# Softmax row sums in an attention sweep: the third pair of probability tiles added on VectorE, and the products with ones run over one tile per batch

## The chip, the cores and the metric

The kernel runs on one core of a Trainium2 chip. The core has five engines with a queue each: TensorE (PE; its weight loads are shown apart as PEld), VectorE (DVE), ScalarE (ACT), GpSimd (POOL) and SyncE (SP), which issues transfers. Each queue works in order, and engines wait for one another through semaphores. The metric is device time in microseconds (us): the median over runs of the whole kernel, which is one launch.

## The reference

One layer of a hybrid backbone: a latent stream of 2048 tokens and a context of 256 tokens, width 1024, in float32. Attention has 8 query heads and 2 key/value heads of size 64; a gated linear recurrence has 4 heads; an output projection and a feed-forward block follow. The change touches the softmax of the latent attention alone:

```python
def latent_attention(qx, kx, vx, kc, vc):
    ...
    keys = jnp.concatenate([kc, kx], axis=1)
    vals = jnp.concatenate([vc, vx], axis=1)
    ...
    def block(q):
        s = jnp.einsum('bqkgd,bnkd->bkgqn', q, keys).astype(jnp.float32) * scale
        p = jax.nn.softmax(s, axis=-1)
        return jnp.einsum('bkgqn,bnkd->bqkgd', p.astype(vals.dtype), vals)
```

Each of 2048 x 8 query rows has 2304 keys. The kernel computes exponentials, multiplies them with the values, sums them per row, and divides at the end. The change is in how the row sums are made.

## The kernel before

The kernel runs in stages: modulation vectors, input projections, the attention sweep with the recurrence woven into it, the output projection, and the feed-forward block. The change lies in the sweep, which takes from about 734 to 1734 us of the profiled span.

**Items and slots.** An `Item` is 128 queries of one key/value group (4 heads, so 512 query columns); there are 32 items. The 2304 keys are 18 key tiles of 128 (`NKT` = 18). The loop at L1098 runs over slots `x`, one for each item and key tile: `n, k = divmod(x, 18)`. In a slot, `scores` computes the scores of one key tile (L1000 and L1001, 128 keys x 512 query columns, into one of three PSUM banks), and ScalarE takes their exponentials into one half of a pair tile `p` of 128x1024 (L1004), two key tiles to a pair. In the same slot `chunk` computes one piece of the score extremes that a later item needs (L969 or L975 on TensorE into one of two PSUM banks, then a minimum on VectorE at L971 or L977).

**Batches.** Six key tiles, which are three pairs, form a batch (`BATCH` = 6): 3 batches an item, 96 in all. In the fourth slot of a batch (`k % 6 == 3`) `add` has GpSimd add the first two pairs into the tile `ps` (L1011). The tile has one buffer. Eight slots after the batch's first one, `products` runs on TensorE: the products of the values with the six tiles (L1020, 12 products, two recorded passes each), accumulated in `av[:, :256]`; then the row sums (L1028), in which a 128x32 tile of ones, `one32`, is multiplied with four blocks of 128 columns for each half of a tile, accumulated in `av[:, 256:384]`. Four such products stand side by side on the array's columns, each on 32 of them. They run over two tiles per batch: the sum `ps`, and the third pair `p`. That is 16 products a batch, in the trace 32 passes. After an item's third batch, `drain` copies `av` out on ScalarE (L1034) and takes the reciprocal of the sums on VectorE (L1036), and `finish` scales the output and writes it to `s_att`.

**The recurrence.** `rec.step` and `rec.round` place the second half of the layer between the slots. A round has, for one or two lanes, small products on TensorE (L684, into `pa`), a masked copy on VectorE (L694), reductions on VectorE (L721), four products on GpSimd (L703, L706, L715, L717) and copies on ScalarE (L709, L710). The round's TensorE part goes ahead of a batch's `products` and its rest behind them (L1190 to L1199).

**The order of the work.** In the sweep the order on TensorE and VectorE is the order of the program text (`manual_schedule`, L1080 and L1159; SyncE too for the first item). The queues of ScalarE and GpSimd, and SyncE's from the second item on, are ordered by a planner that runs a time line of its own when the program is built. So an instruction on VectorE stands exactly where the loop places it, and whatever follows it there waits behind it, while ScalarE's and GpSimd's order may come out differently whenever the program changes.

Of the kernel before, what the change touches and what calls it, by code (L numbers as in the profile page):

```python
# [13 lines left out]
ALU = mybir.AluOpType  # L14
AX = mybir.AxisListType

P = 128
# [36 lines left out]
def rows_bcast(ap, n=P):  # L54

    return bass.AP(tensor=ap.tensor, offset=ap.offset, ap=[[0, n], [1, ap.size()]])
# [12 lines left out]
def block_kernel(ctx: ExitStack, tc: tile.TileContext, a: dict, out: bass.AP, dbg=None):  # L69
    nc = tc.nc  # L70
# [3 lines left out]
    def pool(stack, name, bufs=1, space=None, side=None):  # L74
        kw = dict(name=name, bufs=bufs, reuse_waits="tile", side=side)
        if space is not None:
            kw["space"] = space
        return stack.enter_context(tc.tile_pool(**kw))
# [70 lines left out]
    with ExitStack() as st:  # L149
# [11 lines left out]
        for j in range(8):  # L161
            wm = wmp.tile([P, KT, 256], F32, tag="wm", name=f"wm{j}")
            nc.sync.dma_start(wm, w_mod_r[:, :, j * 256:(j + 1) * 256])
            if j in DVE_MOD:
                for r in range(2):
# [5 lines left out]
                    for i in range(2):  # L171
                        nc.tensor.matmul(pcol[:, 2 * j + i, r:r + 1], acc[:, i * P:(i + 1) * P], ones,
                                         start=True, stop=True)
                continue
            pm = ps_m.tile([P, 512], F32, tag="mm", name=f"pm{j}", bufs=2)
            for k in range(KT):
                nc.tensor.matmul(pm[:2, :256], sc[:, k, :], wm[:, k, :],
                                 start=(k == 0), stop=(k == KT - 1))
# [7 lines left out]
        for r in range(2):  # L186
            for which in range(2):
                ks = slice(which * KT, (which + 1) * KT)
                nc.vector.tensor_tensor(modc[:, 2 * r + 1 - which, :], pcol[:, ks, r], bcol[:, ks],
                                        op=ALU.add)  # L190
# [21 lines left out]
    with ExitStack() as st:  # L212
# [40 lines left out]
        with ExitStack() as p1:  # L253
            ps_x = pool(p1, "ps_x", 4, PSUM)
            xh = pool(p1, "xh", 2)
            for gr in list(range(1, NTOK // 256)) + [0]:
# [6 lines left out]
                b = (gr + 1) // 2  # L263
                o = (gr - 1) % 2 * 256 if gr else 0
# [18 lines left out]
                for kk in range(KT // 2):  # L283
                    pt = ps_x.tile([P, 512], F32, tag="t", name=f"xT{gr}_{kk}")
                    for i in range(2):
                        for j, xt in enumerate(xs):
                            k = 2 * kk + i
# [3 lines left out]
                    for i in range(2):  # L291
                        k = 2 * kk + i
# [317 lines left out]
    with ExitStack() as st:  # L610
# [4 lines left out]
        op = pool(st, "op", 1, side="right")  # L615
# [322 lines left out]
        NKT = NTOK // P  # L938
        BATCH = 6
        LAGT = 3  # L940

        class Item:
# [65 lines left out]
            def add(self, p):  # L1008

                t = self.sums[p // 3] = op.tile([P, 1024], F32, tag="ps", name=f"ps{self.nm}_{p}")  # L1010
                nc.gpsimd.tensor_tensor(t, self.pairs[p - 1], self.pairs[p], op=ALU.add)  # L1011

            def products(self, k0):

                if k0 == 0:
                    self.av = ps_av.tile([P, 512], F32, tag="av", name=f"av{self.nm}")
                for k in range(k0, k0 + BATCH):
                    for i in range(2):
                        o = k % 2 * 512 + i * 256
                        nc.tensor.matmul(self.av[i * 64:(i + 1) * 64, :256],  # L1020
                                         VS[:, k, self.g * 64:(self.g + 1) * 64],
                                         self.pairs[k // 2][:, o:o + 256],
                                         start=(k == 0), stop=(k == NKT - 1), skip_group_check=True)
                b = k0 // BATCH
                for n, t in enumerate((self.sums.pop(b), self.pairs[3 * b + 2])):
                    for o in range(0, 1024, 512):
                        for i in range(4):
                            nc.tensor.matmul(self.av[i * 32:(i + 1) * 32, 256:384], one32,  # L1028
                                             t[:, o + i * P:o + (i + 1) * P], start=False,
                                             stop=(b == 2 and n == 1 and o > 0), skip_group_check=True)  # L1030

            def drain(self):
                self.ot = op.tile([P, 256], F32, tag="ot", name=f"ot{self.nm}")
# [18 lines left out]
        one32 = kvp.tile([P, 32], F32, name="one32")  # L1052
# [9 lines left out]
        def load_kb(g, r):  # L1062
            n = NTOK // 3
            nc.sync.dma_start(f32v(KB[r][:64, :]), s_k[g][:64, r * n:(r + 1) * n])
# [4 lines left out]
        items = [Item(g * NCH + qt, qt, g) for g in range(2) for qt in range(NCH)]  # L1069
# [28 lines left out]
        for x in range(NKT * NIT + 1):  # L1098
            n, k = divmod(x, NKT)
            item = items[n] if n < NIT else None  # L1100
            if item is None:
                rec.begin(2 * NIT)
                assert not chunks and not rec.lanes and not rec.plan and rec.late is None
                items[-1].products(NKT - BATCH)
                items[-1].drain()
                items[-1].finish(ps_st, "s")
                border.close()
                hst.close()
                p5 = ctx.enter_context(ExitStack())
                ep = pool(p5, "ep", 3)  # L1110
                wop = pool(p5, "wop")
                wo = [[wop.tile([P, D], F32R, name=f"wo{w}{k}") for w in "hl"] for k in range(KT)]
                gate1 = wop.tile([P, D], F32, name="gate1")
                mp = pool(p5, "mp", 2)
                wsp = pool(p5, "wsp", 3)
                ps_y = pool(p5, "ps_y", 2, PSUM)
                ps_mt = pool(p5, "ps_mt", 2, PSUM)
                for k in range(KT):
                    ws = wsp.tile([P, D], F32, tag="ws", name=f"wos{k}")
                    nc.sync.dma_start(ws, a["w_out"][0, k * P:(k + 1) * P, :])  # L1120
                    nc.scalar.activation(wo[k][0], ws, AF.Copy)
                    (nc.vector if k in WOV else nc.gpsimd).tensor_tensor(
                        wo[k][1], ws, f32v(wo[k][0]), op=ALU.subtract)
                nc.sync.dma_start(gate1, rows_bcast(modrow[0, 2 * D:3 * D]))

                mixed = {}

                def mix_token(t):

                    rw = slice(t * P, (t + 1) * P)  # L1130
                    mx = mp.tile([P, D], F32, tag="mix", name=f"mix{t}")
                    for g in range(2):
                        nc.sync.dma_start(mx[:, g * 256:(g + 1) * 256].rearrange("p (c t) -> p c t", t=P),
                                          s_att[g][:, rw].rearrange("(c p) t -> p c t", p=P))
                    for h in range(NH):
                        nc.sync.dma_start(mx[:, 512 + h * P:512 + (h + 1) * P], s_hg[h][rw, :])
                    mh = mp.tile([P, KT, P], F32R, tag="mh", name=f"mh{t}")
                    ml = mp.tile([P, KT, P], F32R, tag="ml", name=f"ml{t}")
                    pt = ps_mt.tile([P, 512], F32, tag="t", name=f"mt{t}")
                    for i in range(4):  # L1140
                        nc.tensor.transpose(pt[:, i * P:(i + 1) * P], mx[:, 512 + i * P:512 + (i + 1) * P], ident)
                    for kk, (src, eng) in enumerate(((mx[:, :512], nc.gpsimd), (pt, nc.vector))):
                        pv = src.rearrange("p (k t) -> p k t", t=P)
                        nc.scalar.activation(mh[:, kk * 4:kk * 4 + 4, :], pv, AF.Copy)
                        eng.tensor_tensor(ml[:, kk * 4:kk * 4 + 4, :], pv,
                                          f32v(mh[:, kk * 4:kk * 4 + 4, :]), op=ALU.subtract)
                    mixed[t] = mh, ml

                mix_token(NCH // 2)
                break  # L1150
            if n == NCH - 1 and k in (8, 14):
                load_kb(1, k // BATCH - 1)
            if n == NCH and k == 0:
                load_kb(1, 2)
            if x == NKT:
                nc.sync.dma_start(f32v(KS[1]), s_k[1])
            if x == NKT:
                border.close()
                border.enter_context(tc.manual_schedule(engines={mybir.EngineType.PE, mybir.EngineType.DVE}))  # L1159
            if k == 6 and n + 2 < NIT:  # L1160
                items[n + 2].load()
            if k == 4 and n + 1 < NIT:
                items[n + 1].load_low()
            item.scores(k)
            if k == 3 and n:
                items[n - 1].drain()
            for m, c in chunks.pop(x, ()):
                items[m].chunk(c)
            if rec.late is not None:
                wait -= 1  # L1170
                if wait <= 0:
                    rec.flush()
            made = iter(())
            for hr, j in STEPS.get(k, ()):
                hr += 2 * n
                if j == 0 and hr:
                    rec.begin(hr)
                rec.step(hr, j)
                if (hr, j) in outputs:
                    wait = 3  # L1180
                if j != 5:
                    next(rec.beside, 0)
                else:
                    made = rec.round()
            if k == 13 and n + 1 < NIT:
                items[n + 1].maxima()
            if k == 5 and n:
                items[n - 1].finish(ps_h, "h")
            pending.append(made)
            if k % BATCH == LAGT - 1:  # L1190
                made = [m for m in pending]
                pending.clear()
                for m in made:
                    next(m, 0)
                y = x - LAGT + 1 - BATCH
                if y >= 0:
                    items[y // NKT].products(y % NKT)
                for m in made:
                    next(m, 0)  # L1199
# [593 lines left out]
```

## Time and profile before

| what | us |
|---|---|
| median of 3 runs | 3235.79 |
| lowest and highest of them | 3234.75, 3237.18 |
| profiled execution, its own time | 3230.49 |
| span of that execution | 3228.7 |
| mean granted TensorE clock in it | 0.993 |

The profiled execution is a run by itself, 5.3 us under the median; 1.8 us of its own time lie outside the span.

How to read the rows. A row of the busy times has for each engine the busy time, its share of the span and the number of instructions. A row of a stretch has its start and end, its length, and then for PE, PEld, DVE, ACT and POOL the busy time and the number of instructions; then the granted TensorE clock, the share of the DMA engines and GB/s. Where such a row is of one engine alone, it has that engine's busy time only. A row of a time line has the start, the time from its first start to its last end, the engine, the line, the operation, output and inputs with their shapes, and how many instructions are merged in it; in brackets stands idle time before it and what ended that. A row of waits names who waited for whom, the total, how often, and the longest. A row of one source line has the shortest, median and longest duration in ns. Names stand without buffer numbers: `ps` is the sum tile, `p` a pair, `mn` the minima, `mx` their scores, `pa` the recurrence's products, `one` the ones. TensorE's matmuls are pipelined, so that neighbouring rows of it overlap.

### The profile page before, as it was taken

Reading aid. Unit: us, or ns where it says so; the run is one execution under the profiler, and the core shown is the slowest. Engines: PE = TensorE matmul, PEld = TensorE weight load, DVE = VectorE, ACT = ScalarE, POOL = GpSimd, SP = SyncE. Lnnn points to the kernel's source line nnn. Section 1 sums busy time; section 2 is a strip of 40 time slices with the busy share of each in tenths; the row PEclk is TensorE's granted clock in tenths of the full one; section 3 lists DMA queues with packets and bytes.
Section 4 is the critical chain, followed back from the end, with each engine's and each line's share of the span. In section 5 each row is a group of like instructions: output and inputs, shape, how many; then the busy total and the mean of one; then the engine's idle time right before and its main releaser. Section 6 shows DMA issues by size and latency. Waiting matters only on the chain. (4 is left out here: it accounts for less than half of the span.)

```text
span 3228.7 us, 55815 instructions
## 1 busy us (share of the span) xinstructions
PE 3145.3 (97%) x21212; PEld 2559.5 (79%) x21212; DVE 1755.1 (54%) x3070; ACT 1326.6 (41%) x2563; POOL 1575.1 (49%) x1403
## 2 busy tenths in 40 slices
PE   8999999999999999999999999999999999999998
PEld 5998987896777777777777887888877778888886
DVE  6344555416666665665653656445458753333566
ACT  4422222215554555554543225333335443333344
POOL 4322222206767767776634226777600168776222
PEclk9999999999999999999999999999999999999999
DMA  7243544324111211211006435555575533332665
GB/s 246 92 137 125 153 145 146 119 93 121 31 36 46 67 34 49 59 37 48 28 21 201 134 115 183 196 179 189 173 291 195 193 111 115 108 104 98 243 195 185
DMA packets 368999, 406.86 MB, mean 126 GB/s; under 512 B 31285, under 2 KB 260889, under 8 KB 368346
## 3 DMA queue, kind: packets, MB, share of 16 engines
q1 hardware_dynamic: 368730, 403.30, 38.9%
q8 instruction: 166, 2.72, 0.4%
q14 instruction: 103, 0.84, 0.1%
HBM read 273.34 MB, written 129.78 MB: 125 GB/s over the span
## 5 line engine op out<-in xcount | busy, mean ns | idle before, releaser
L971 DVE TENSOR_REDUCE mn<-mx 128x1 f32<-128x512 f32 x496 | 333.9, 685 | 209.7 <-PE mx L969 204.6
L1004 ACT ACTIVATE p<-s 128x512 f32<-128x512 f32 x576 | 338.5, 598 | 167.3 <-PE s L1001 147.5
L1011 POOL TENSOR_TENSOR ps<-p,p 128x1024 f32<-128x1024 f32 x96 | 229.9, 2395 | 162.3 <-ACT p L1004 162.3
L1020 PE MATMUL av<-p,VS 128*64 128x256 f32 x2304 | 268.7, 382 | 0.0
L1000 PE MATMUL s<-qa,K 128*128 128x512 f32 x576 | 253.4, 440 | 10.8 <-ACT p L1004 10.8
L1001 PE MATMUL s<-qb,KB 128*128 128x512 f32 x576 | 227.4, 395 | 0.0
L1020 PEld LDWEIGHTS av<-p,VS 128*64 128x64 f32 x2304 | 158.9, 138 | 82.5 <-issue 13.9
L969 PE MATMUL mx<-K,qa 128*128 128x512 f32 x496 | 200.9, 406 | 2.7 <-DVE mn L971 2.4
L1621 DVE TENSOR_TENSOR dl<-dl,x 128x512 fp32r<-128x512 f32 x154 | 113.7, 761 | 70.8 <-ACT x L1614 69.9
L1000 PEld LDWEIGHTS s<-qa,K 128*128 128x128 f32 x576 | 109.0, 189 | 47.9 <-issue 19.8
L1614 ACT ACTIVATE x<-dl 128x512 fp32r<-128x512 f32 x154 | 96.2, 631 | 106.1 <-DMA dl<-s_hid0A 41.1
L1614 ACT ACTIVATE dh<-dl 128x512 fp32r<-128x512 f32 x154 | 89.0, 623 | 93.7 <-PE pd1A L1682 48.3
L345 PE MATMUL f<-hTh,wh 128*128 128x512 f32 (+1 forms) x320 | 120.8, 377 | 6.9 <-ACT ft L374 6.9
L969 PEld LDWEIGHTS mx<-K,qa 128*128 128x128 f32 x496 | 93.4, 188 | 41.4 <-DVE mn L971 17.8
L1621 DVE TENSOR_TENSOR dl<-dl,dh 128x512 fp32r<-128x512 f32 x154 | 102.0, 688 | 43.1 <-ACT dh L1614 42.0
L122 POOL TENSOR_TENSOR rs_xf<-ms_xf,mhalf 128x1 f32<-128x1 f32 x16 | 12.7, 803 | 227.6 <-DVE ms_xf L120 227.6
L345 PE MATMUL f<-hTh,wl 128*128 128x512 f32 (+1 forms) x320 | 118.5, 370 | 0.0
L345 PE MATMUL f<-hTl,wh 128*128 128x512 f32 (+1 forms) x320 | 118.4, 370 | 0.0
L1001 PEld LDWEIGHTS s<-qb,KB 128*128 128x128 f32 x576 | 109.6, 190 | 10.9
L1445 PE MATMUL pA<-x,A22h 128*128 128x512 f32 x352 | 108.9, 391 | 4.5 <-DVE r L1518 4.5
L1445 PE MATMUL pA<-x,A11h 128*128 128x512 f32 x352 | 110.7, 395 | 2.4 <-ACT A11h L1414 2.4
L1445 PE MATMUL pC<-x,A12h 128*128 128x512 f32 x352 | 112.0, 391 | 0.0
(373 smaller groups left out, 9337.0 us busy)
## 6 DMA issues: line engine op xcount, KB each, us to landing
w<-in_w_gu_dram SPq DMA_DIRECT2D x88, 512.0 KB
wm<-in_w_mod_dram SPq DMA_DIRECT2D x24, 1024.0 KB
dl<-s_wT SPq DMA_DIRECT2D x88, 256.0 KB
dl<-s_wB SPq DMA_DIRECT2D x66, 256.0 KB
wq<-in_w_down_dram SPq DMA_DIRECT2D x44, 256.0 KB
s_wT<-wq SPq DMA_DIRECT2D x44, 256.0 KB
dl<-s_hid1S SPq DMA_DIRECT2D x44, 256.0 KB
dl<-s_hid0S SPq DMA_DIRECT2D x44, 256.0 KB
```

The lines of the kernel that those rows point to most:

```text
L122: nc.gpsimd.tensor_tensor(rs, ms, mhalf[:, :width], op=ALU.pow)
L345: nc.tensor.matmul(pm[:, :n], w[wi][:, k, c0:c0 + P], hT[b][hi][:, k, :], start=(k == 0 and i == 0), stop=(k == KT - 1 and i == 2))
L969: nc.tensor.matmul(s, self.qa[:, h * P:(h + 1) * P], K[:, k * 512:(k + 1) * 512], start=True, stop=True)
L971: nc.vector.tensor_reduce(self.mn[:, h, k:k + 1], s, axis=AX.X, op=ALU.min)
L1000: nc.tensor.matmul(s, KS[self.g][:, ks], self.qa, start=True, stop=False)
L1001: nc.tensor.matmul(s, KB[k // BATCH][:, k % BATCH * P:(k % BATCH + 1) * P], self.qb, start=False, stop=True)
L1004: nc.scalar.activation(self.pairs[p][:, o:o + 512], s, AF.Exp, scale=-1.0)
L1011: nc.gpsimd.tensor_tensor(t, self.pairs[p - 1], self.pairs[p], op=ALU.add)
L1020: nc.tensor.matmul(self.av[i * 64:(i + 1) * 64, :256], VS[:, k, self.g * 64:(self.g + 1) * 64], self.pairs[k // 2][:, o:o + 256], start=(k ...
L1445: nc.tensor.matmul(acc, w[wi][:, k, :], x[xi][k], start=(start and k == 0 and i == 0), stop=(stop and k == KH - 1 and i == 2), skip_group_ ...
L1614: nc.scalar.activation(hi, f32v(lo), AF.Copy)
L1621: nc.vector.tensor_tensor(lo, f32v(lo), f32v(hi), op=ALU.subtract)
```

## The change

A method `add_last` adds the third pair to the sum tile in place, on VectorE. `products` then runs the ones products over that one tile: 8 products a batch instead of 16. In the loop `add_last` is placed in slots with `k % 6 == 1`, behind the slot's `scores` and `chunk` and ahead of the recurrence's step; for a batch whose first slot is k0 that is slot k0 + 7, one slot ahead of its `products`. For the last item's last batch it stands directly ahead of `products` behind the loop. The tiles, their buffers and all other instructions stay.

```diff
+            def add_last(self, p):
+
+                t = self.sums[p // 3]
+                nc.vector.tensor_tensor(t, t, self.pairs[p], op=ALU.add)
+
             def products(self, k0):
...
                 b = k0 // BATCH
-                for n, t in enumerate((self.sums.pop(b), self.pairs[3 * b + 2])):
-                    for o in range(0, 1024, 512):
-                        for i in range(4):
-                            nc.tensor.matmul(self.av[i * 32:(i + 1) * 32, 256:384], one32,
-                                             t[:, o + i * P:o + (i + 1) * P], start=False,
-                                             stop=(b == 2 and n == 1 and o > 0), skip_group_check=True)
+                t = self.sums.pop(b)
+                for o in range(0, 1024, 512):
+                    for i in range(4):
+                        nc.tensor.matmul(self.av[i * 32:(i + 1) * 32, 256:384], one32,
+                                         t[:, o + i * P:o + (i + 1) * P], start=False,
+                                         stop=(b == 2 and o > 0), skip_group_check=True)
...
                 assert not chunks and not rec.lanes and not rec.plan and rec.late is None
+                items[-1].add_last(NKT // 2 - 1)
                 items[-1].products(NKT - BATCH)
...
             for m, c in chunks.pop(x, ()):
                 items[m].chunk(c)
+            if k % BATCH == 1 and x > BATCH:
+                items[(x - 2) // NKT].add_last((x - 2) % NKT // 2)
             if rec.late is not None:
```

## The prediction

> **What bounds the kernel now.** I read the page's busy times and its chain of waits first, then the table by stretches for the attention sweep, then its groups of instructions.
>
> ```profile
> PE 3145.3 (97%) x21212; PEld 2559.5 (79%) x21212; DVE 1755.1 (54%) x3070; ACT 1326.6 (41%) x2563; POOL 1575.1 (49%) x1403
> 734.00:1734.00 1000.00, 975.51 (x10051) 727.90 (x10051) 597.31 (x1067) 515.49 (x1042) 678.65 (x715) 0.99 0.18 53
> DVE mn L971 <- PE mx L969: 188.3, 106, 4.0
> POOL ps L1011 <- ACT p L1004: 162.3, 51, 8.6
> PEld s L1000 <- ACT p L1004: 16.4, 17, 2.8
> PE s L1000 <- ACT p L1004: 10.8, 8, 2.4
> PEld mx L969 <- DVE mn L971: 15.5, 38, 1.0
> ```
>
> The second row is the whole sweep, from 734 to 1734 us: TensorE is busy for 975.5 of 1000 us at a granted clock of 0.99, VectorE for 597, ScalarE for 515, GpSimd for 679. The last five rows are waits of that stretch (total, times, longest). VectorE and GpSimd mostly wait for work that TensorE leads; TensorE's own waits are small: 27 us for ScalarE's exponentials, 15.5 us for VectorE's minima. So TensorE's instruction stream sets the length of this stage, and time taken out of it counts, unless another engine then becomes late.
>
> **What is removed.** Per batch, eight products of `one32` with the third pair: 16 recorded passes.
>
> ```profile
> L1028 PE MATMUL av<-ps,one x1536: 272/273/298, 743.5 to 1733.6; 128*32 128x128 f32 x192
> L1028 PE MATMUL av<-p,one x1536: 272/273/273, 744.0 to 1734.0; 128*32 128x128 f32 x192
> 743.53 0.64 PE L1028 MATMUL av<-ps,one 128*32 128x128 f32 x16
> 744.00 0.62 PE L1028 MATMUL av<-p,one 128*32 128x128 f32 x16
> 744.54 0.50 PE L1000 MATMUL s<-qa,K 128*128 128x512 f32 x1
> ```
>
> 1536 / 16 = 96 batches. The passes overlap (273 ns each, but 16 of them in 0.62 us), so a group is priced from its start to the next group's start. The step from the group over the sum tile to the group over the third pair is 0.46 to 0.47 us here and in the rows below; the next step, 0.54 us, also holds the change back to the wide score product, which stays. I take 0.46: 96 x 0.46 = **44.2 us** off TensorE.
>
> **What is added.** 96 additions of 128x1024 on VectorE, both inputs in SBUF. Weight preparation after the sweep has the same shape:
>
> ```profile
> L1122 DVE TENSOR_TENSOR wol<-wos,woh x4: 1225/1226/2959, 1720.1 to 1737.6; 128x1024 fp32r<-128x1024 f32 x4
> 1720.12 2.96 DVE L1122 TENSOR_TENSOR wol<-wos,woh 128x1024 fp32r<-128x1024 f32 x1 [6.89 <-ACT woh L1121]
> 1719.62 5.71 POOL L1122 TENSOR_TENSOR wol<-wos,woh 128x1024 fp32r<-128x1024 f32 x2
> ```
>
> 1.23 us undisturbed, so 96 x 1.23 = 118 us of VectorE's 403 idle us. One of the four took 2.96 us: it began while GpSimd was in a subtraction over SBUF. So the price has two ends, 1.23 us alone and 2.96 us behind such an operation.
>
> [...]
>
> **Where the addition lies in a usual batch.** It stands on VectorE behind the minimum of slot k0 + 7 and ahead of that of slot k0 + 8 (k0 is the batch's first key tile). This is a whole batch on three engines:
>
> ```profile
> 1361.54 0.40 PE L969 MATMUL mx<-K,qa 128*128 128x512 f32 x1
> 1362.26 0.50 PE L969 MATMUL mx<-K,qa 128*128 128x512 f32 x1
> 1362.69 1.17 PE L684 MATMUL pa<-Q,M 128*64 128x64 f32 x32
> 1363.69 2.76 PE L1020 MATMUL av<-p,VS 128*64 128x256 f32 x24
> 1366.38 0.64 PE L1028 MATMUL av<-ps,one 128*32 128x128 f32 x16
> 1366.84 0.62 PE L1028 MATMUL av<-p,one 128*32 128x128 f32 x16
> 1367.96 0.39 PE L969 MATMUL mx<-K,qa 128*128 128x512 f32 x1
> ...
> 1361.52 1.97 DVE L971 TENSOR_REDUCE mn<-mx 128x1 f32<-128x512 f32 x3
> 1363.90 0.74 DVE L694 COPY_PREDICATED A<-mask,pa 128x512 f32<-128x512 int32 x1 [0.41 <-PE pa L684]
> 1365.30 0.67 DVE L721 TENSOR_REDUCE T<-T 128x256 f32<-128x512 f32 x1
> 1368.39 0.69 DVE L971 TENSOR_REDUCE mn<-mx 128x1 f32<-128x512 f32 x1 [2.42 <-PE mx L969]
> ...
> 1363.47 0.65 POOL L715 TENSOR_TENSOR Q<-Q,T 128x256 f32<-128x256 f32 x1 [2.93 <-PE pa L684]
> 1368.90 2.40 POOL L1011 TENSOR_TENSOR ps<-p,p 128x1024 f32<-128x1024 f32 x1
> 1363.47:1371.30 7.83, 7.83 (x9) 1.00 0.00 0
> ```
>
> Two of the three minima are done at 1361.52 + 2/3 x 1.97 = 1362.83. GpSimd is idle there, so the addition runs to 1364.06. The ones products want it at 1366.38: 2.3 us to spare, under the value products of L1020. Queued behind it are the third minimum (then done at 1364.75) and the recurrence's masked copies and reductions, 2.07 us from 1363.90 to 1365.97 before and so to 1366.8 after. The next minimum is ready for VectorE at 1368.39, or 1367.93 with TensorE 0.46 us earlier. So 1.1 us remain: the addition costs nothing here. The cover is VectorE's 2.42 us wait during the products; with no cover it costs 1.23 - 0.46 = 0.77 us net per batch.
>
> GpSimd's L715 is held from 1363.47 to 1364.06, 0.6 us, and by the last row (a stretch of 7.83 us, all of it busy, in nine operations) its queue runs without a pause to the end of the next `ps` sum, which so comes 0.6 us later. What GpSimd does late, ScalarE and the next addition receive late.
>
> **Where it doesn't fit.** The addition needs GpSimd's sum of the first two pairs. By the wait row above, 51 of the 96 sums waited for exponentials; the other 45 started behind GpSimd's own queue. Two of those:
>
> ```profile
> 787.01 2.38 POOL L1011 TENSOR_TENSOR ps<-p,p 128x1024 f32<-128x1024 f32 x1
> 786.40 1.38 DVE L971 TENSOR_REDUCE mn<-mx 128x1 f32<-128x512 f32 x2
> 789.73 0.64 PE L1028 MATMUL av<-ps,one 128*32 128x128 f32 x16
> ...
> 1088.55 2.38 POOL L1011 TENSOR_TENSOR ps<-p,p 128x1024 f32<-128x1024 f32 x1
> 1090.89 0.86 POOL L715 TENSOR_TENSOR Q<-Q,T 128x256 f32<-128x256 f32 x1
> 1089.38 1.28 DVE L971 TENSOR_REDUCE mn<-mx 128x1 f32<-128x512 f32 x2
> 1090.58 0.76 DVE L694 COPY_PREDICATED A<-mask,pa 128x512 f32<-128x512 int32 x1
> 1092.43 0.18 DVE L721 TENSOR_REDUCE T<-T 128x16 f32<-128x32 f32 x1
> 1093.05 0.64 PE L1028 MATMUL av<-ps,one 128*32 128x128 f32 x16
> 1095.06 4.15 DVE L971 TENSOR_REDUCE mn<-mx 128x1 f32<-128x512 f32 x6 [2.45 <-PE mx L969]
> ```
>
> First one: the sum is done at 789.39, VectorE stands from 787.09, the addition ends at 790.62, and the ones products, wanted at 789.73, are 0.89 us late.
>
> Second one: VectorE is free at 1090.07, the sum is done at 1090.93, but GpSimd is already in L715 until 1091.75. The addition then ends at 1092.98, just in time for 1093.05. Behind it, though, stand a minimum (0.69) and the recurrence's work, 2.03 us from 1090.58 to 1092.61: done at 1095.7, where the next minimum was due at 1095.06 - 0.46 = 1094.6. VectorE is 1.1 us behind, and its six minima in 4.15 us are 0.69 us each, the same as TensorE's slot (the products for the minima of 1361.54 and 1362.26 above are 0.72 us apart), so it does not catch up before the next products. With two banks for the minima some 0.3 us of that is forgiven (4.15 / 6 a slot, two slots, less matmul and reduction): 0.8 us on TensorE.
>
> So such a batch costs 0 (the one at 1368.90 is also of the 45 and has its products as far off as the first batch shown) to 0.85 us, the mean of 0.89 and 0.8. All 45 would make 38 us. I take a third, 13 us, because most recurrence rounds leave the 2.4 us wait. The waits for exponentials (25 in all, 27 us) could each grow by GpSimd's 0.6 us: 0 to 15 us; I take 2, near the lower end, because GpSimd has its own pauses (162 us ahead of `ps`) in which such a delay ends. The first item has no output to drain and the last no minima; both go at the same price. At the end of the sweep the last addition may be held by L1122 on GpSimd (2.96 - 1.23 = 1.7 us, once); output projections fill TensorE there, so nothing. Transfers don't move.
>
> **Sum.** -44.2 + 13 + 2 = -29 us: the profiled span 3228.7 becomes 3200, its own time 3230.5 becomes 3201.5, and the median of the runs shown, 3235.8, becomes **3207 us**. With the bounds of the unknown terms, 0 to 53, the time lies between 3192 and 3245.
>
> **Rivals.** (1) Nothing is lost: 3235.8 - 44.2 = 3192. For it: 2.3 us to spare in the usual batch. Against: the 45 late sums.
>
> (2) A new wait takes the place of the products: all 45 late batches cost 0.85 us and the exponentials 2: -44.2 + 40 = -4, 3232, which can't be told from no change (0.2%, 6.5 us, is about what a measurement here can tell). For it: 0.89 us worked out at 789. Against: VectorE idles 40% of the stage.
>
> [...]
>
> **Chances.** Forecast 0.52 (its own range 3196 to 3226), rival 1 0.20, rival 2 0.11, rival 3 0.17. Rival 2 I count as 0.03 faster, 0.07 same, 0.01 slower; of the forecast's 0.52, a tail of 0.02 lies within 0.2%. Faster: 0.50 + 0.20 + 0.03 = 0.73; same 0.09; slower 0.18. The range runs from 3188, a little under rival 1, to 3244, the end of the bounds; most of rival 3 is left out.
>
> **What would show it.** [...] A TensorE wait for `ps` on VectorE of some 0.9 us in many batches would be rival 2. If the sweep shrinks by 44 us with the same waits, rival 1 holds. The forecast is wrong if the sweep's 1000 us shrink by less than 15.

## The result, and the profile after

The changed kernel takes 3237.89 us in the median of 12 runs (3229.09 to 3246.02), the kernel before 3235.28 in 12 runs beside it (3230.74 to 3241.61). The ratio is 1.0009 with a 95% interval of 0.9996 to 1.0022: no change that can be told, where 3207 was forecast. The profiled execution of the changed kernel is the shortest of its runs, 3229.09 us; what follows is read from it and holds for the pattern, not for the last few microseconds.

The table by stretches, the changed kernel's sweep (columns as for the stretch shown of before):

```profile
734.00:1734.00 1000.00, 951.12 (x8546) 695.19 (x8545) 717.01 (x1165) 510.08 (x1039) 714.33 (x713) 0.98 0.18 52
```

TensorE is busy for 24 us less in these 1000 us than before (975.51), VectorE for 120 us more, and GpSimd, of which the change asks nothing new, for 36 us more (678.65 before). The waits of that stretch:

```profile
PEld s L1000 <- ACT p L1004: 29.4, 25, 3.4
PE s L1000 <- ACT p L1004: 21.8, 13, 3.0
PEld mx L969 <- DVE mn L971: 15.2, 36, 1.0
DVE ps L1016 <- POOL ps L1011: 15.1, 20, 2.0
...
PE pk L732 <- POOL M L703: 8.8, 3, 2.9
...
PEld av L1033 <- DVE ps L1016: 3.6, 6, 1.0
```

TensorE's waits for exponentials doubled (10.8 to 21.8 us), three waits of up to 2.9 us for GpSimd are new, the waits for VectorE's minima stayed at 15.2 us, and the waits for the added-to sum tile are small. (A row of PEld, the loads, and one of PE, the products, are in part of the same moments, so such rows can't be added.) The time went to waits that end with ScalarE and GpSimd, not with VectorE.

The single lines of the changed kernel (shortest, median and longest in ns): the addition, and one of GpSimd's recurrence products,

```profile
L1016 DVE TENSOR_TENSOR ps<-ps,p x96: 1212/1216/3159, 736.5 to 1723.8; 128x1024 f32<-128x1024 f32 x96
...
L715 POOL TENSOR_TENSOR Q<-Q,T x96: 612/804/1836, 764.6 to 1645.4; 128x256 f32<-128x256 f32 x96
```

and the same product in the kernel before:

```profile
L715 POOL TENSOR_TENSOR Q<-Q,T x96: 617/664/876, 769.0 to 1653.4; 128x256 f32<-128x256 f32 x96
```

The shortest are alike; the longest grew from 0.88 to 1.84 us, by 0.96 us, most of an addition. GpSimd's operations are being held.

**Where in the sweep.** I compared batch by batch the step from the start of one batch's first score product (L1000) to the next batch's. From the first score product to the last, the sweep is 1.0 us shorter than before. That is 59 batches that gain 0.38 to 0.50 us each, 25.3 us together; 19 batches that lose more than 0.3 us each, 35.3 us together; and 11.0 us of gains in the other 18. The losses come back every 21 batches (numbered from 0: 27, 48 and 69 lose 5.1 to 5.2 us each; 35/36, 56/57 and 77/78 some 3.4 us a pair), and at the start and the end. At the first kind the recurrence hands over from one set of units to the next: its last L703/L706 round fills the tiles that TensorE transposes in L732. The time line of the changed kernel there (one of three alike):

```profile
970.65 2.38 POOL L1011 TENSOR_TENSOR ps<-p,p 128x1024 f32<-128x1024 f32 x1
...
973.06 1.46 DVE L1016 TENSOR_TENSOR ps<-ps,p 128x1024 f32<-128x1024 f32 x1 [1.64 <-POOL ps L1011]
973.40 1.82 POOL L706 TENSOR_TENSOR C<-M,T 128x128 f32<-128x128 f32 x2
...
979.66 0.42 ACT L709 ACTIVATE M<-C 128x256 f32<-128x256 f32 x1 [0.93 <-POOL M L703]
979.99 0.58 ACT L1004 ACTIVATE p<-s 128x512 f32<-128x512 f32 x1
...
980.62 0.50 PE L1000 MATMUL s<-qa,K 128*128 128x512 f32 x1 [2.60 <-ACT p L1004]
...
981.54 2.35 POOL L1011 TENSOR_TENSOR ps<-p,p 128x1024 f32<-128x1024 f32 x1
...
983.84 0.63 POOL L703 TENSOR_TENSOR M<-M,T 128x256 f32<-128x256 f32 x1
...
984.52 0.47 PE L732 MATMUL pk<-identr,M 128*128 128x128 f32 x1 [2.94 <-POOL M L703]
...
985.29 0.78 PE L1000 MATMUL s<-qa,K 128*128 128x512 f32 x1
```

The same place in the kernel before, 8 us later on its clock, with GpSimd's row of a stretch (length, busy time and count, granted clock):

```profile
973.00:991.00 18.00, 17.92 (x26) 1.00 0.09 29
...
980.00 0.50 POOL L703 TENSOR_TENSOR M<-M,T 128x128 f32<-128x128 f32 x1
980.41 0.89 POOL L706 TENSOR_TENSOR C<-M,T 128x128 f32<-128x128 f32 x2
...
987.23 0.42 ACT L709 ACTIVATE M<-C 128x256 f32<-128x256 f32 x1 [1.09 <-POOL M L703]
987.56 0.58 ACT L1004 ACTIVATE p<-s 128x512 f32<-128x512 f32 x1
987.74 0.62 POOL L703 TENSOR_TENSOR M<-M,T 128x256 f32<-128x256 f32 x1
988.19 0.50 PE L1000 MATMUL s<-qa,K 128*128 128x512 f32 x1 [1.62 <-ACT p L1004]
...
988.67 2.39 POOL L1011 TENSOR_TENSOR ps<-p,p 128x1024 f32<-128x1024 f32 x1
```

GpSimd is busy for 17.92 of 18 us here: it has no slack, and TensorE already waits for it, by way of ScalarE. ScalarE's copy L709 waits for GpSimd's L703, the exponential L1004 stands behind that copy in ScalarE's queue, and the score product needs the exponential's bank: 987.23, 987.56, 988.19. After the change, GpSimd's L706 is held under the addition (two take 1.82 us; the same two took 0.89 before), and the planner put the `ps` sum of 2.35 us ahead of the last L703, so the transposes wait 2.94 us (run 2 below separates the two). Then the score product takes 0.78 us in place of 0.50. The table by stretches shows that it runs at a lower clock; TensorE, its loads, VectorE, ScalarE, GpSimd, then the granted clock:

```profile
983.10:989.90 6.80, 5.38 (x20) 3.85 (x22) 2.51 (x3) 4.65 (x10) 4.35 (x7) 0.50 0.00 0
```

Half the clock for 6.8 us. In the sweep such stretches of 3.4 or 6.8 us come to 13.7 us before and 41.0 us after.

### The profile page after: what moved, and what is told of

Read it like the earlier page. It is cut to its first block, busy times and chain, and to the rows that moved or that the text cites. A ratio compares the mean times of both kernels' runs of the same rounds, so it can differ in the third digit from the quotient of the medians.

```text
span 3227.2 us, 53006 instructions
## 1 busy us (share of the span) xinstructions
PE 3118.3 (97%) x19676; PEld 2524.0 (78%) x19676; DVE 1875.1 (58%) x3166; ACT 1322.5 (41%) x2563; POOL 1615.3 (50%) x1403
## 5 line engine op out<-in xcount | busy, mean ns | idle before, releaser
L1004 ACT ACTIVATE p<-s 128x512 f32<-128x512 f32 x576 | 334.9, 596 | 168.3 <-PE s L1001 152.3
L1000 PE MATMUL s<-qa,K 128*128 128x512 f32 x576 | 257.4, 447 | 24.4 <-ACT p L1004 24.3
L1000 PEld LDWEIGHTS s<-qa,K 128*128 128x128 f32 x576 | 110.5, 192 | 64.0 <-ACT p L1004 32.3
L1016 DVE TENSOR_TENSOR ps<-ps,p 128x1024 f32<-128x1024 f32 x96 | 135.6, 1413 | 20.7 <-POOL ps L1011 15.1
L715 POOL TENSOR_TENSOR Q<-Q,T 128x256 f32<-128x256 f32 x96 | 79.7, 830 | 79.4 <-PE pa L684 79.4
```

The lines of the kernel that those rows point to most:

```text
L1000: nc.tensor.matmul(s, KS[self.g][:, ks], self.qa, start=True, stop=False)
L1004: nc.scalar.activation(self.pairs[p][:, o:o + 512], s, AF.Exp, scale=-1.0)
```

## The experiments

Two explanations stood at the start: the planner's new order of GpSimd and ScalarE (theory O), and the addition itself (theory H). To separate them, an order could be imposed: the places of each engine's instructions are taken from the other kernel and written down as ordering-only dependencies, in runs 1 to 7 and 9 (8 and 10 have the planner's own order):

```diff
+        mark0 = len(list(nc.all_instructions()))
...
+                swept = list(nc.all_instructions())[mark0:]
+                for eng, order in ORDERS.items():
+                    own = [i for i in swept if i.engine == eng]
...
+                    for m, n in zip(order, order[1:]):
+                        tc.add_manual_dep(own[n], own[m].name, mybir.DependencyInfo(
+                            mybir.DependencyClass.NoSync, mybir.DependencyReason.DATA), reason="order")
```

The results of all ten, beside the kernel before on the same chip (3230.8, 3233.2 and 3230.1 us in the three sets). "Sweep" is the first to the last score product in the profiled execution against before's; "half clock" is the time at a granted clock of 0.5 in it. Both come from one execution each, which can lie off its kernel's median: the change's is its shortest run, 8.8 us under it, and run 1's is its longest, 5.0 us over it.

| run | median us | difference | ratio (95%) | sweep | half clock |
|---|---|---|---|---|---|
| 1 change, order of before | 3226.69 | -4.1 | 0.9989 (0.998 to 0.9998) | -0.6 | 27.3 |
| 2 before, order of the change | 3236.52 | +5.7 | 1.0019 (1.0009 to 1.0028) | +3.2 | 17.1 |
| 3 fewer products, no addition | 3206.23 | -24.6 | 0.9926 (0.9911 to 0.994) | -24.2 | 20.5 |
| 4 addition, all products | 3259.42 | +28.6 | 1.0095 (1.0077 to 1.0113) | +25.7 | 23.9 |
| 5 maximum in the addition's place | 3235.52 | +2.4 | 1.0005 (0.9996 to 1.0014) | +2.1 | 10.2 |
| 6 addition that waits for no sum | 3261.72 | +28.6 | 1.0087 (1.0074 to 1.0101) | +19.8 | 23.9 |
| 7 change in 70 batches, order of before | 3213.28 | -19.9 | 0.9941 (0.9929 to 0.9953) | -17.7 | 20.5 |
| 8 change in 70 batches, planner's order | 3206.09 | -27.1 | 0.9917 (0.9904 to 0.9931) | -26.0 | 10.2 |
| 9 run 3 without 14 sums | 3194.22 | -35.9 | 0.9892 (0.988 to 0.9905) | -39.3 | 6.8 |
| 10 run 8 without 14 sums | 3203.76 | -26.3 | 0.9923 (0.9911 to 0.9935) | -28.2 | 6.8 |

**1 and 2: the order alone.** The change with GpSimd's and ScalarE's order of before, and the kernel before with the order that the planner made for the change; no other edit.

> The change as it is, but GpSimd's 712 and ScalarE's 1035 instructions of the sweep are kept in the order that they have in the kernel before. Theory O (what the products gave was lost because the planner reordered GpSimd and ScalarE): the ratio to before is 0.985 to 0.992, about 3190 to 3210 us; the steps of 5 us at the hand-over batches are gone and TensorE has half-clock stretches as before, about 14 us in the sweep. [...]

> The kernel before without the change, but GpSimd and ScalarE are kept in the order that the planner gave them for the changed kernel. Theory O: slower than before by 20 to 45 us, ratio 1.006 to 1.014, with TensorE stalled at the recurrence's transposes as in the changed kernel. Theory H: the order is harmless without the addition, ratio 0.998 to 1.003.

Both move by some 6 us from the kernel with its own order: run 1 is at -4.1 where the change itself has +2.6 (3237.89 - 3235.28), run 2 at +5.7. With the order held, the change gains little in either: -4.1 us in the order of before, and 2.6 - 5.7 = -3.1 in its own. So the order counts, but it isn't where 30 us went. It does make part of the hand-overs. Run 2 has no addition, and its transposes wait as in the changed kernel (8.8 us in three waits there too):

```profile
PE pk L732 <- POOL M L703: 8.8, 3, 3.0
```

Its batches 27, 48 and 69 lose 4.8, 4.7 and 3.2 us, and most of that comes back elsewhere, 1.5 us each in 26, 47 and 68. In run 1 these three waits are gone. The wait for an exponential just ahead of the transposes grows with the change in either order: from 1.62 us (before) to 4.10 (run 1), and from 0.5 (run 2, TensorE's loads only) to 2.60 (the changed kernel). So that growth comes with the change, and the transposes' wait with the order.

**3 and 4: the two halves of the change.** Run 3 makes the eight products over `ps` alone and no addition (the third pair is left out of the row sums, and the reciprocal reads a part of the value products). Run 4 makes the addition and keeps all sixteen products (the third pair counts twice). Both in the order of before.

```diff
-                items[(x - 2) // NKT].add_last((x - 2) % NKT // 2)
...
-                nc.vector.reciprocal(self.li, self.av[:, 256:384])
+                nc.vector.reciprocal(self.li, self.av[:, 128:256])
```

```diff
-                t = self.sums.pop(b)
+                for n, t in enumerate((self.sums.pop(b), self.pairs[3 * b + 2])):
```

> Half of the change, in the order of before: the ones products run over the sum tile alone and nothing is added on VectorE, so the third pair is left out of the row sums (and the reciprocal reads 128 columns of the value products instead). Both theories: the whole 44 us less than before, 3186 to 3196 us, ratio 0.985 to 0.988; a rival, that the removed products lay under other waits, gives 0.993 or more. What e1 is above this is the price of the addition in the old order: O says 0 to 15 us, H 35 to 45 us.

> The other half alone, in the order of before: the addition on VectorE is made, and the ones products still run over both tiles, so the third pair counts twice in the row sums. Theory O: 0 to 10 us above before, ratio 1.000 to 1.003, since the addition lies in VectorE's wait. Theory H: 30 to 50 us above before, ratio 1.009 to 1.016.

The two halves add up roughly: -24.2 + 25.7 = +1.5 us in the sweep, where the whole change in this order has -0.6, but -24.6 + 28.6 = +4.0 in the medians, where it has -4.1. On top of run 3, the addition costs 20.5 us (run 1), outside what either theory gave. Run 3 misses its expected 3186 to 3196 us, and run 4 lies just under the 30 us of theory H. Both halves differ from the sum of the prediction. The products' removal brings 24.6 us and not 44.2: 63 batches gain 0.38 to 0.50 us each (27.1 us), 11 lose 11.5 us, eight of them at the hand-overs (5/6, 26/27, 47/48, 68/69) and three at the start and the end, and the rest gain 8.5 us. The addition costs 28.6: 64 batches change by less than 0.1 us, and 19 carry 25.2 of the 25.7 us. Where they lie fits GpSimd's slack. In the kernel before, GpSimd is busy for 99 to 100% of nine batches, 5, 8, 14, 26, 35, 47, 56, 68 and 77, and of the last one, 95, but for at most 86% of any other; two of the nine (5 and 35) as GpSimd's rows of a stretch:

```profile
774.27:784.60 10.33, 10.33 (x18) 1.00 0.04 10
1086.18:1096.26 10.08, 10.08 (x12) 1.00 0.01 2
```

Of the 19 batches that lose, 16 are these nine or stand next to one, with 20.0 of the 25.2 us; the other three are 1, 92 and 95, at the start and the end. By this the places in the middle of a cycle (34/35, 55/56, 76/77) are of one kind with the hand-overs.

**5 and 6: what in the addition costs.** Either GpSimd is held off while VectorE adds from two tiles (H1), or VectorE stands in its queue until GpSimd's sum is there (H2). Run 5 puts a maximum over `ps` in the addition's place: as long, behind the same wait, one input. Run 6 adds the third pair to itself, into a scratch tile: two inputs, no wait for the sum. All sixteen products stay, and nothing of the computation is changed in either.

```diff
-                nc.vector.tensor_tensor(t, t, self.pairs[p], op=ALU.add)
+                r = sm.tile([P, 1], F32, tag="junk", name=f"junk{self.nm}_{p}")
+                nc.vector.tensor_reduce(r, t, axis=AX.X, op=ALU.max)
```

```diff
-                nc.vector.tensor_tensor(t, t, self.pairs[p], op=ALU.add)
+                t = op.tile([P, 1024], mybir.dt.bfloat16, tag="junk", name=f"junk{self.nm}_{p}")
+                nc.vector.tensor_tensor(t, self.pairs[p], self.pairs[p], op=ALU.add)
```

> Kernel before with one more VectorE instruction per batch in the addition's place: a maximum over the sum tile (128x1024 to 128x1, one SBUF input), which waits for GpSimd's sum as the addition does; all products stay, GpSimd's and ScalarE's order of before. The same with the real addition cost +28.6 us. [...] Theory H2 (VectorE stands in its queue until GpSimd's sum is there, and what is behind it on VectorE comes late): the cost stays at +20 us or more.

> Kernel before with one more VectorE instruction per batch in the same place: the third pair added to itself into a scratch bfloat16 tile (128x1024, two SBUF inputs), which doesn't wait for GpSimd's sum; all products stay, GpSimd's and ScalarE's order of before. [...] H2 (wait): the cost vanishes, 0 to +8 us. If both this and the maximum cost some 10 to 20 us, both parts count; if neither costs, it takes both together (a late start that then meets GpSimd).

VectorE's wait costs nothing that can be told (run 5), and the two-input instruction without it costs 28.6 us (run 6). Two limits stay. In runs 5 and 6 TensorE's products don't wait for the new instruction; in run 4 they do, for 4.3 us in six batches, and its sweep is 5.9 us longer than run 6's. And in the profiled execution of run 6, 19.8 us of the cost lie in the sweep and 10.8 behind the last score product, with a half clock of 37.0 us there against 19.2 before; apart from the last batch's products no kernel changes the code there, and that part of the span differs from before by -0.4 to +10.8 us in the eleven others' profiles, so how much of the 10.8 belongs to the addition stays open. The time line of the same hand-over in run 4 (addition),

```profile
982.11 1.46 DVE L1016 TENSOR_TENSOR ps<-ps,p 128x1024 f32<-128x1024 f32 x1 [1.27 <-POOL ps L1011]
982.42 1.85 POOL L706 TENSOR_TENSOR C<-M,T 128x128 f32<-128x128 f32 x2
...
991.15 0.79 PE L1000 MATMUL s<-qa,K 128*128 128x512 f32 x1 [3.47 <-ACT p L1004]
```

in run 5 (maximum),

```profile
980.11 1.22 DVE L1017 TENSOR_REDUCE junk<-ps 128x1 f32<-128x1024 f32 x1 [0.37 <-POOL ps L1011]
980.43 0.85 POOL L706 TENSOR_TENSOR C<-M,T 128x128 f32<-128x128 f32 x2
...
988.17 0.50 PE L1000 MATMUL s<-qa,K 128*128 128x512 f32 x1 [1.59 <-ACT p L1004]
```

and in run 6 (two inputs, no wait):

```profile
976.83 2.40 POOL L1011 TENSOR_TENSOR ps<-p,p 128x1024 f32<-128x1024 f32 x1
977.92 2.38 DVE L1016 TENSOR_TENSOR junk<-p 128x1024 bf16<-128x1024 f32 x1
979.16 1.46 POOL L703 TENSOR_TENSOR M<-M,T 128x128 f32<-128x128 f32 x1
...
988.31 0.79 PE L1000 MATMUL s<-qa,K 128*128 128x512 f32 x1 [3.48 <-ACT p L1004]
```

Under the addition two L706 take 1.85 us; under a maximum of 1.22 us, as long as an addition alone and begun as far ahead of them, 0.85. In run 6 both take turns: the addition, ready in the middle of GpSimd's sum, ends 1.1 us after it (2.38 us in place of 1.2), and the L703 behind the sum is held in its turn (1.46 us; the same one took 0.50 before). TensorE's wait grows from 1.6 to 3.5 us in runs 4 and 6 alike, and the score product after it runs at the low clock. Over the whole kernel the held product L715 says the same, in run 5 and in run 6:

```profile
L715 POOL TENSOR_TENSOR Q<-Q,T x96: 620/665/879, 768.9 to 1655.2; 128x256 f32<-128x256 f32 x96
```

```profile
L715 POOL TENSOR_TENSOR Q<-Q,T x96: 612/794/1843, 766.4 to 1668.5; 128x256 f32<-128x256 f32 x96
```

Run 6 differs from run 5 in a full-size output too, so the runs don't tell the second input from the output. Nor do they show what the two engines take turns at: what was measured is that L706 took 1.85 us under the addition and 0.85 under the maximum.

**9: why the products' removal brought only 24.6 us.** If GpSimd's full queue paces the hand-overs, TensorE's saved time is no gain there. Run 9 is run 3 with less for GpSimd: in 14 batches about the hand-overs its sum is left out, and the eight products run over the third pair instead.

```diff
+        DROP = {b for b in range(84) if b % 21 in (3, 4, 5)} | {91, 94}
...
-                if k % BATCH == 3:
+                if k % BATCH == 3 and 3 * self.n + k // BATCH not in DROP:
                     self.add(p)
...
-                t = self.sums.pop(b)
+                t = self.sums.pop(b, self.pairs[3 * b + 2])
```

> The kernel that showed -24.6 us (products of ones over one tile per batch, no addition, division by a part of the value products in place of the row sums, order of before), and in 14 batches (of every 21 the 4th, 5th and 6th, and 91 and 94) GpSimd's sum of the first two pairs is left out too; there the eight products run over the third pair. TensorE's work is the same. If GpSimd's full queue sets the pace at the recurrence's hand-overs (theory), the missing 20 us come back for the most part: -34 to -44 us against before, ratio 0.9865 to 0.9895, and TensorE's waits for exponentials of 2.5 us there fall under 1 us. If ScalarE's queue or the recurrence's own chain of steps sets it (rival), nothing or little is gained: -24 to -29, ratio 0.991 to 0.993.

It came out at the lower edge of the first range, -35.9 us, and in the sweep at -39.3 us: 15 of the missing 20 us came back there, and 11 in the medians. The hand-over in run 3,

```profile
978.92 0.42 ACT L709 ACTIVATE M<-C 128x256 f32<-128x256 f32 x1 [1.08 <-POOL M L703]
...
979.88 0.50 PE L1000 MATMUL s<-qa,K 128*128 128x512 f32 x1 [2.47 <-ACT p L1004]
...
981.03 0.72 PE L1000 MATMUL s<-qa,K 128*128 128x512 f32 x1
```

and in run 9 (its source lines stand one further down):

```profile
976.14 0.42 ACT L709 ACTIVATE M<-C 128x256 f32<-128x256 f32 x1 [1.09 <-PE s L1001]
...
977.10 0.50 PE L1001 MATMUL s<-qa,K 128*128 128x512 f32 x1 [0.52 <-ACT p L1005]
...
978.25 0.48 PE L1001 MATMUL s<-qa,K 128*128 128x512 f32 x1
```

In run 3 TensorE arrives earlier than before and waits 2.47 us in place of 1.62: 0.85 us of what it saved is handed back at once, and the longer stall is followed by the low clock (0.50 for 3.4 us, with 0.72 us for a score product), which costs up to 1.7 us more (an estimate: half of 3.4). With GpSimd relieved the wait is 0.52 us and the clock stays up. The batches 26, 27, 47, 48, 68 and 69, which lose 0.4 to 1.2 us each in run 3, gain 0.42 to 1.55 us each in run 9.

**7 and 8: a version that uses it.** The change is made in 70 batches only; in the 26 in which run 4 showed a cost, or just ahead of those, sixteen products stay and no addition is made.

```diff
+        KEEP = {b for b in range(84) if b % 21 in (3, 4, 5, 12, 13)} | {7, 8, 82, 91, 94, 95}
...
             def add_last(self, p):
+                if 3 * self.n + p // 3 in KEEP:
+                    return
...
-                t = self.sums.pop(b)
+                tiles = [self.sums.pop(b)] + ([self.pairs[3 * b + 2]] if 3 * self.n + b in KEEP else [])
```

> The change made in 70 of the 96 batches only; the 26 at and ahead of the recurrence's hand-overs (of every 21 batches the 4th, 5th, 6th, 13th and 14th, and 7, 8, 82, 91, 94, 95) keep sixteen products of ones and get no addition; GpSimd's and ScalarE's order of before. If the loss sits in those hand-overs: 70 x 0.44 = -31 us at best, ratio 0.990 to 0.994, faster than before and than the whole change, with half-clock time back near 14 us. If the addition costs the same in every batch (70/96 of the +28.6 stays): -31 + 21 = -10 us, ratio 0.997 or above.

> The same 70 batches, GpSimd and ScalarE ordered by the planner as it comes out. If the order is worth the 6 to 7 us that the whole change and the kernel before showed when their orders were exchanged: 6 us above the one with the order of before, ratio 0.992 to 0.996. If the planner puts the sums ahead of the recurrence's products again: hand-overs of +5 us each (three of them), ratio 0.996 to 1.000.

Run 8 is 27.1 us faster than before, 0.9917 (0.9904 to 0.9931), of 70 x 0.44 = 31 us that were to be had. Run 7, with the order of before, has 19.9: my expectation that the old order would be the better one by 6 us was wrong. The planner's order gains 1.4 us each at the batches 23, 44 and 65, where the old one loses 0.3 to 0.5; against that, at one hand-over of three (68/69) it loses 2.7 us, where the old one loses 2.0. So the order of before, with its faster hand-overs there, isn't the better one for another stream of TensorE. Run 8's sweep and its waits:

```profile
734.00:1734.00 1000.00, 971.31 (x9057) 718.33 (x9057) 689.84 (x1159) 517.15 (x1054) 701.25 (x719) 0.99 0.20 59
```

```profile
PEld mx L970 <- DVE mn L972: 15.9, 38, 1.0
PEld s L1001 <- ACT p L1005: 12.9, 15, 3.2
PE s L1001 <- ACT p L1005: 10.6, 8, 2.8
```

The waits for exponentials are back at the 10.8 us of before, and TensorE is busy for 971 us of the 1000 again.

**10: the sums left off GpSimd in a full computation.** Run 8, and in the 14 batches of run 9 GpSimd makes no sum; the products of ones run over all three pairs there.

```diff
-                tiles = [self.sums.pop(b)] + ([self.pairs[3 * b + 2]] if 3 * self.n + b in KEEP else [])
+                m = 3 * self.n + b
+                tiles = [self.pairs[3 * b], self.pairs[3 * b + 1]] if m in DROP else [self.sums.pop(b)]
+                if m in KEEP:
+                    tiles.append(self.pairs[3 * b + 2])
```

> The change in 70 of 96 batches as in the selective kernel that showed 0.9917; of the other 26, 14 have no sum on GpSimd either: their products of ones run over all three pairs, 24 instead of 16. The planner's own order; nothing of the computation is left out. TensorE gets 14 x 0.46 = 6.4 us more, GpSimd 14 x 2.4 = 34 us less. If GpSimd sets the pace at the hand-overs: the 6.4 us lie in waits that are there anyway, and some 3 x 3 us or more come back, ratio 0.986 to 0.991. If not: 0.992 to 0.994.

A miss: 0.9923 can't be told from run 8. The hand-overs did get freer (TensorE's waits for exponentials at 27, 48 and 69 fall from 1.60, 1.60 and 2.79 us in run 8 to 0.81 each; 26 and 47 gain 0.34 to 0.37 us against before), but in run 8 only one of the three still lost time, 68/69, and the eight more products cost 0.41 to 0.46 us in 25, 27, 46, 48, 67 and 69, where TensorE leads once GpSimd is out of the way. What one engine was given the other paid for.

## Why the prediction was wrong, by its own steps

**"TensorE's instruction stream sets the length of this stage."** This is the step that failed. It is true in 59 of the 96 batches, which gain 0.38 to 0.50 us, as the 0.46 said. It is wrong at the recurrence's hand-overs, where GpSimd's full queue sets the length, and both terms of the sum go wrong there. I read it from a sum over 1000 us, in which TensorE waits 27 us for exponentials, and called that small. The 27 us also count moments twice: the loads' 17 waits and the products' 8 are in part the same (at 988.19 us a load waits 2.02 and the product 1.62 us), and the products stood for 10.8 us. So the 25 waits behind the bound of 15 us were 17 at most. They are few and long, 1.6 us at the hand-overs, and they are the places in which another engine leads.

**The term -44.2 us.** Mis-sized by its first factor, the 96 batches; this is the larger miss, 19.6 us. The removal alone measured -24.6 us (run 3), and -39.3 us of sweep when GpSimd was relieved at the hand-overs (run 9).

**The addition, 13 + 2 us.** Here the mechanism failed too. The cost of one addition alone, 1.23 us, was right (shortest and median 1.212 and 1.216), and the mean of the 96 is 1.41 us. The 13 us were for late sums: VectorE waits for GpSimd, is late with the minima, and holds TensorE. That mechanism hardly appeared. TensorE's waits for minima went from 15.5 to 15.2 us, and run 5, with the same wait in the same place, costs nothing that can be told. Late sums reached TensorE's products for 0.7 us in the change and 4.3 us in run 4, where the batch worked out at 789 us with 0.89 us waited 0.91. The 2 us were for GpSimd being held (the 0.6 us of L715), set near the lower end "because GpSimd has its own pauses". The kernel before shows such a hold, behind a subtraction of the weight preparation that has the addition's size:

```profile
1727.53 1.23 DVE L1122 TENSOR_TENSOR wol<-wos,woh 128x1024 fp32r<-128x1024 f32 x1 [2.81 <-ACT woh L1121]
1728.12 2.88 POOL L1011 TENSOR_TENSOR ps<-p,p 128x1024 f32<-128x1024 f32 x1 [1.54 <-ACT p L1004]
```

GpSimd's sum, begun 0.59 us behind the subtraction's start, took 2.88 us, the longest of the 96, where their median is 2.39. GpSimd has its pauses in the batch that I looked at; at the hand-over it is busy for 17.92 of 18 us. There a hold of about 1 us reaches TensorE, whose wait grows from 1.6 to 3.5 us in run 6, and a half-clock stretch comes with the stall. Run 6, which has this hold and no late sum, costs 28.6 us, 19.8 of them in the sweep: beyond the term's upper bound of 15. The right mechanism was in the text, with the wrong price, because it was priced in one usual batch. So the result lies inside the range that ended at 3244 by luck: that end was made mostly of late sums, and they weren't what came.

**The rivals.** Rival 2's outcome, no change, is what came out, but not by its mechanism: the products of ones waited 0.7 us in two batches for the addition, their loads 3.6 us in six, not 0.9 us in many. Rival 3's outcome, a slower kernel, did not come: GpSimd's lateness, which is the cause, reaches TensorE in 19 batches, with 64 untouched (run 4). By the sign given for a wrong forecast, a sweep that shrinks by less than 15 us, it was wrong: 1.0.

**The planner's order**, for which the sum has no term, is worth about 6 us here (runs 1 and 2). It puts the `ps` sum ahead of the last L703 at the three hand-overs, which makes most of the 5.1 to 5.2 us that one batch loses there; run 2 loses 3.2 to 4.8 in the same batches without any addition.

What stays open: how much of the loss at a hand-over is the stall and how much the low clock. The 41.0 - 13.7 = 27.3 us of additional half clock are at most 13.6 us of lost work (an estimate: half of them, if TensorE had work throughout), so the clock alone isn't the whole of it; in run 4 it is 10.2 us more, at most 5.1 of its 25.7 us. No run kept the stall and took away the low clock.

## What to carry to other kernels

GpSimd, busy for 68% of this stage, is busy for 17.92 of 18 us in the middle of it; look for the stretches in which each engine has no slack, and price an edit there, not in a typical batch. The wait that shows it can name another engine: TensorE's waits here read as waits for ScalarE's exponentials, because ScalarE's queue has a copy ahead of them that waits for GpSimd. An addition of two 128x1024 tiles on VectorE beside GpSimd's work lengthened both here (run 6: the addition 2.38 us in place of 1.2, GpSimd's L703 1.46 in place of 0.50), and in this kernel it hurts where GpSimd paces the rest; put such an edit only where it costs nothing, as the 70 batches here did, chosen by run 4's losses, for 0.9917. An expected gain is the sum over those places where the relieved engine leads, and a longer stall of TensorE there can cost more than was saved (run 3: six hand-over batches lost 0.4 to 1.2 us each).

## What the runs showed of the hardware

The granted clock of TensorE halved in or behind most of the stalls of over 2 us. In the sweeps of the twelve profiles, none of 51 stalls of TensorE's products of 1.0 to 1.7 us had a half-clock stretch begin between its start and 4 us after its end, but 60 of 91 stalls of over 2.0 us had (0 of 8 and 16 of 20 in the profiles of before and of the change); 57 of the 58 stretches begin so. Each stretch lasted 3.4 or 6.8 us; the score products shown above in one took 0.72 to 0.79 us in place of 0.50. 52 of those 60 stalls were of 2.1 to 3.0 us.

The hold went both ways: in run 6 the addition that became ready during GpSimd's sum took 2.38 us in place of 1.2, and the next GpSimd operation, L703, 1.46 us in place of 0.50.
